# Down projection of a decoder layer: VectorE's order in the fifth and sixth product, and the place of the residual loads

## The chip, the cores and the metric

The kernel runs on one core of a Trainium2 chip. A core has five engines that run on their own and meet only at semaphores: TensorE (PE, matrix products; PEld is its loading of weights), VectorE (DVE), ScalarE (ACT), GpSimd (POOL) and SyncE (SP), which here issues most of the transfers (DMA) between the chip's main memory and the on-chip buffers. The metric is the time of one execution on the device in microseconds; lower is better. Each engine takes its instructions in one written order, so an instruction that waits holds up everything that stands behind it on the same engine.

## The reference, cut to what matters

The layer mixes tokens in two branches (RWKV-7 and S5) and then runs a gated MLP. Only the end of the MLP is touched here: the down projection, the norm behind it, and the residual.

```python
def conv_ffn(h, w_up, conv_w, conv_b, w_down):
    ...
    return (jax.nn.gelu(gate) * val) @ w_down
...
        f = conv_ffn(h, ffn_w_up[l], ffn_conv_w[l], ffn_conv_b[l], ffn_w_down[l])
        x = x + rms_norm(f, norm_ffn_post[l])
```

The hidden width is 2816, the model width 1024, and there are 1024 tokens, all in float32.

## The kernel before, in words

**Seven products.** `down` computes the projection as a two-by-two block product with seven block products instead of eight (Strassen's scheme in Winograd's form). The weights are cut into halves of the hidden width (`kh`, 11 tiles of 128 each) and of the output width (`mh`, 512 columns each), the activations into the same halves of the hidden width and halves of the tokens (`th`, 512 each). The products run in the order `p1, p2, p5, p6, p7, p4, p3`: so p7 is the **fifth product** and p4 the **sixth**, and p3 the seventh. Sums and differences of blocks that the scheme needs are built by VectorE, group by group (`add`, `sub`, lines 1566 and 1569).

**Groups.** Each product runs over the 11 tiles in six groups (`DGROUPS`): two tiles in each, but one tile in the third. A group of two tiles has operands of 128x1024 and 24 matmuls, the half group 128x512 and 12. A product has 132.

**Three matmuls for one.** Every operand is split into a high part (a cast by ScalarE, line 226: `wh` for weights, `xh` for activations) and a low part (VectorE subtracts the cast from the original, line 227: `wl`, `xl`). `step` then issues `xh*wh` (line 1614), `xl*wh` (1615) and `xh*wl` (1616). The operand buffers form a ring of three: the casts of a group wait until TensorE has left the group three before.

**Staging.** Blocks that are needed once are loaded into a ring of four staging buffers (`st`): weight blocks by `a_` (line 1539), activation blocks by `b_` (line 1545). In the fifth product each group loads two, a weight block and an activation block, and VectorE subtracts both (`st<-A,st` and `st<-B,st`) before they are split. A staging buffer is free again when the low part has been taken from it, so the load for a group goes out when `wl` or `xl` of the group two before is done. In the sixth product each group loads two weight blocks: one is split, the other is used by VectorE for `S<-st,S`, an operand of the seventh product.

**Residual.** `resid(th)` loads the residual in eight pieces of 256 KB for each half of the tokens (line 1651): into buffers `T` for the first half, into buffers `A` for the second, as these come free. `outputs` (lines 1660 to 1662) scales, adds the residual and stores; for the first half it runs within the seventh product, for the second after it.

**What sets the order.** TensorE's instructions stay in the order in which they are written. For the other engines a scheduler orders them by its own estimate of when each can start. SP issues all the transfers spoken of here, in one queue and in that order.

Of the kernel before, what the change touches and what calls it, by code (L numbers as in the profile page):

```python
# [9 lines left out]
F32 = mybir.dt.float32  # L10
# [3 lines left out]
ALU = mybir.AluOpType  # L14
# [52 lines left out]
class Kern:  # L67
# [156 lines left out]

    def split(self, hi, lo, x, eng=None):
        self.nc.scalar.copy(hi, x)  # L226
        (eng or self.nc.vector).tensor_tensor(lo, x, hi.bitcast(F32), ALU.subtract)  # L227

    def split_half(self, hi, lo, x, eng=None):

# [1287 lines left out]
    def down(self, dq0, dqf, dqt, dqa, dqs, dqb):  # L1518
# [3 lines left out]
        nc, V, A = self.nc, self.nc.vector, self.nc.scalar  # L1522
        mm = nc.tensor.matmul
        HF = FT // 2
# [3 lines left out]
        def wide(pool, tag, dt=F32, bufs=1):  # L1528
            return pool.tile([128, 1024], dt, tag=tag, name=self.nm(tag), bufs=bufs)

        def cache(tag, g):
            n = len(groups[g])
            pool = {"A": dq0 if g < 4 else dqt, "T": dqt, "S": dqa, "B": dqa if g < 3 else dqb}[tag]
            return pool.tile([128, 512 * n], F32, tag=f"{tag}{g}", name=self.nm(tag), bufs=1)

        def a_(t, mh, kh, g):

            for q, k in enumerate(groups[g]):
                nc.sync.dma_start(t[:, q * 512:q * 512 + 512], self.a["w_down"][kh * HF + k][:, mh * 512:mh * 512 + 512])
            return t  # L1540

        def b_(t, kh, th, g):
# [11 lines left out]
        def operands(g, a, b):  # L1554
            r = ring[0] % 3
            ring[0] += 1
            n = 512 * len(groups[g])
            pool = dqt if r else dq0
            w = [wide(pool, f"w{c}{r}", F32R)[:, :n] for c in "hl"]
            x = [wide(pool, f"x{c}{r}", F32R)[:, :n] for c in "hl"]  # L1560
            self.split(*w, a)
            self.split(*x, b)
            return w, x

        def add(o, x, y):
# [5 lines left out]
        def p1(g):  # L1571
            cA[g], b, cT[g] = a_(cache("A", g), 0, 0, g), b_(stage(g), 0, 0, g), b_(cache("T", g), 0, 1, g)
            o = operands(g, cA[g], b)
            sub(cT[g], cT[g], b)
            return o

        def p2(g):
            o = operands(g, a_(stage(g), 0, 1, g), b_(stage(g), 1, 0, g))
            cS[g] = a_(cache("S", g), 1, 0, g)
            return o  # L1580

        def p5(g):
            add(cS[g], cS[g], a_(stage(g), 1, 1, g))
            o = operands(g, cS[g], cT[g])
            cB[g] = b_(cache("B", g), 1, 1, g)
            sub(cT[g], cB[g], cT[g])
            return o
# [23 lines left out]
        def step(op, q, m, ps, start, stop):  # L1611
            (wh, wl), (xh, xl) = op
            c, x = slice(q * 512 + m * 128, q * 512 + m * 128 + 128), slice(q * 512, q * 512 + 512)
            mm(ps, wh[:, c], xh[:, x], start=start, stop=False, skip_group_check=True)  # L1614
            mm(ps, wh[:, c], xl[:, x], start=False, stop=False, skip_group_check=True)  # L1615
            mm(ps, wl[:, c], xh[:, x], start=False, stop=stop, skip_group_check=True)  # L1616

        def bank(m):
            return self.ps.tile([128, 512], F32, tag=f"d{m}", name=self.nm("d"), bufs=1)

        def product(prep, ps, first, evict, between=lambda g: None):

            for g in range(ng):
                op = prep(g)
                n = len(groups[g])
                qm = [(q, m) for q in range(n) for m in range(4)]
                if g in (0, ng - 1):
                    qm = [(q, m) for m in range(4) for q in range(n)]
                for q, m in qm:
                    step(op, q, m, ps[m], first and g == 0 and q == 0, g == ng - 1 and q == n - 1)  # L1630
                    if g == ng - 1 and q == n - 1:
                        evict(m)
                between(g)
# [9 lines left out]
            acc[th] = sq  # L1643

        def resid(th):
            xs = []
            for m in range(0, NK, 2):
                t = cache("T" if th == 0 else "A", (0, 1, 3, 4)[m // 2])
                for q in range(2):
                    x = t[:, q * 512:q * 512 + 512]  # L1650
                    nc.sync.dma_start(x, self.X1[(m + q) * 128:(m + q) * 128 + 128, th * 512:th * 512 + 512])
                    xs.append(x)
            return xs
# [11 lines left out]
        b, x = [bank(m) for m in range(4)], [bank(4 + m) for m in range(4)]  # L1665
# [33 lines left out]
        def middle(g):  # L1699
            if g == 0:  # L1700
                ss = bank(0)
                self.sumsq(ss, acc[0], True)
                d["y"] = self.rstd(ss, 1e-6, 1.0 / D)
                d["xs"] = resid(0)
            elif g == 1:
                bc = bank(1)
                self.spread(bc, d["y"])
                d["bc"] = dq0.tile([128, 512], F32, tag="bc", name=self.nm("bc"), bufs=1)
                A.copy(d["bc"], bc)
            elif g == 3:  # L1710
                d["xs1"] = resid(1)
        d, last = {}, []
        product(p1, b, True, keep1)
        product(p2, x, True, c11)
        product(p5, x, True, lambda m: None)
        product(p6, b, False, keep2)
        product(p7, b, False, c22)
# [279 lines left out]
```

## Time and profile before

| | |
|---|---|
| timed runs | 1488.09, 1490.83, 1492.19 us; median 1490.83 |
| profiled execution, first to last instruction | 1491.1 us |
| TensorE busy | 1435.8 us (96%) |
| VectorE busy | 1071.2 us (72%) |
| ScalarE busy | 729.8 us (49%) |
| mean granted TensorE clock | 0.984 |
| seven products of the down projection | 1254.9 to 1473.4 us |

For the profiled execution no time other than its span is given; it lies 0.3 us above the median of the runs. Line numbers such as L1569 are those of the kernel before. A wait is read as "engine and line that waited <- engine and line that released it". Names carry no buffer numbers in the profile: `st` is any staging buffer, `d` any of the accumulators of the down projection. A matmul row shows its own length of 0.39 us, but matmuls overlap, so the pace is read from the distance of their starts.

### The profile page before, as it was taken

Reading aid. Unit: us, or ns where it says so; the run is one execution under the profiler, and the core shown is the slowest. Engines: PE = TensorE matmul, PEld = TensorE weight load, DVE = VectorE, ACT = ScalarE, POOL = GpSimd, SP = SyncE. Lnnn points to the kernel's source line nnn. Section 1 sums busy time; section 2 is a strip of 40 time slices with the busy share of each in tenths; the row PEclk is TensorE's granted clock in tenths of the full one; section 3 lists DMA queues with packets and bytes.
Section 4 is the critical chain, followed back from the end, with each engine's and each line's share of the span. In section 5 each row is a group of like instructions: output and inputs, shape, how many; then the busy total and the mean of one; then the engine's idle time right before and its main releaser. Section 6 shows DMA issues by size and latency. Waiting matters only on the chain. (4 is left out here: it accounts for less than half of the span.)

```text
span 1491.1 us, 24155 instructions
## 1 busy us (share of the span) xinstructions
PE 1435.8 (96%) x9284; PEld 1176.3 (79%) x9284; DVE 1071.2 (72%) x1761; ACT 729.8 (49%) x1167; POOL 58.9 (4%) x116
## 2 busy tenths in 40 slices
PE   7999999999999989899999999999999999999996
PEld 5778888778878778677878877888888887888785
DVE  8977765665325859646597798777777777697677
ACT  7677653443324553633554455444444444443351
POOL 0000000010100110100000000000000000000001
PEclk9999999999999999899999999999999999999998
DMA  6453433633511575733374643222222227934723
GB/s 217 121 194 116 129 94 91 212 113 122 164 59 58 171 226 163 189 109 108 121 222 150 205 127 121 85 85 85 85 85 81 76 70 260 328 125 133 236 83 113
DMA packets 121284, 206.26 MB, mean 138 GB/s; under 512 B 29248, under 2 KB 35520, under 8 KB 121168
## 3 DMA queue, kind: packets, MB, share of 16 engines
q1 hardware_dynamic: 113296, 182.43, 39.2%
q0 software_dynamic: 6144, 19.99, 4.0%
q10 hardware_dynamic: 1728, 2.29, 0.4%
q8 instruction: 73, 1.20, 0.4%
q14 instruction: 43, 0.35, 0.1%
HBM read 150.14 MB, written 52.43 MB: 136 GB/s over the span
## 5 line engine op out<-in xcount | busy, mean ns | idle before, releaser
L172 PE MATMUL gm<-hh,wh 128*128 128x512 f32 x672 | 277.0, 412 | 10.5 <-DVE ev L1192 4.3
L173 PE MATMUL gm<-hl,wh 128*128 128x512 f32 x672 | 265.4, 395 | 0.0
L174 PE MATMUL gm<-hh,wl 128*128 128x512 f32 x672 | 265.2, 395 | 0.0
L156 ACT CAST wh<-wf 128x512 fp32r<-128x512 f32 x171 | 105.6, 619 | 168.3 <-PE gm L173 103.8
L157 DVE TENSOR_TENSOR wl<-wf,wh 128x512 fp32r<-128x512 f32 x171 | 116.9, 686 | 77.6 <-ACT wh L156 77.3
L172 PEld LDWEIGHTS gm<-hh,wh 128*128 128x128 f32 x672 | 127.6, 190 | 42.8 <-issue 5.9
L174 PEld LDWEIGHTS gm<-hh,wl 128*128 128x128 f32 x672 | 128.0, 190 | 28.1
L173 PEld LDWEIGHTS gm<-hl,wh 128*128 128x128 f32 x672 | 128.2, 191 | 24.7 <-issue 1.0
L1615 PE MATMUL d<-xl,wh 128*128 128x512 f32 x308 | 121.4, 394 | 3.5 <-DVE xl L227 3.5
L1614 PE MATMUL d<-xh,wh 128*128 128x512 f32 x308 | 121.4, 394 | 2.1 <-ACT xh L226 2.1
L1616 PE MATMUL d<-xh,wl 128*128 128x512 f32 x308 | 121.2, 393 | 0.0
L1440 PE MATMUL rp<-t,h 128*128 128x512 f32 x216 | 84.4, 391 | 1.6 <-ACT p L1454 1.6
L1442 PE MATMUL rp<-t,l 128*128 128x512 f32 x216 | 84.2, 390 | 0.5 <-DVE l L227 0.5
L1441 PE MATMUL rp<-t,h 128*128 128x512 f32 x216 | 84.1, 389 | 0.0
L1615 PEld LDWEIGHTS d<-xl,wh 128*128 128x128 f32 x308 | 58.6, 190 | 16.5 <-DVE xl L227 4.3
L1614 PEld LDWEIGHTS d<-xh,wh 128*128 128x128 f32 x308 | 58.5, 190 | 14.8 <-ACT xh L226 2.5
L1616 PEld LDWEIGHTS d<-xh,wl 128*128 128x128 f32 x308 | 58.6, 190 | 12.2
L226 ACT CAST h<-r 128x1024 fp32r<-128x1024 f32 x34 | 35.8, 1054 | 61.1 <-PE rp L1441 29.6
L227 DVE TENSOR_TENSOR l<-r,h 128x1024 fp32r<-128x1024 f32 x34 | 41.6, 1224 | 29.2 <-ACT h L226 27.7
L1461 DVE SCALAR_TENSOR_TENSOR y<-zv,vecs,y 128x1023 f32<-128x1023 f32 (+1 forms) x36 | 46.1, 1280 | 8.5 <-ACT y L1459 8.5
L1440 PEld LDWEIGHTS rp<-t,h 128*128 128x128 f32 x216 | 40.5, 188 | 11.2 <-ACT p L1454 2.5
L1454 ACT COPY p<-rp 128x512 f32<-128x512 f32 x54 | 31.0, 574 | 36.5 <-PE rp L1442 36.5
(459 smaller groups left out, 3199.4 us busy)
## 6 DMA issues: line engine op xcount, KB each, us to landing
r<-in_w_up_dram SPq DMA_DIRECT2D x36, 512.0 KB, 3.7
wf<-in_w_in_dram SPq DMA_DIRECT2D x62, 256.0 KB, 3.1
st<-in_w_down_dram SPq DMA_DIRECT2D x55, 256.0 KB, 4.1
st<-ACT SPq DMA_DIRECT2D x44, 256.0 KB, 4.5
wf<-in_w_up_dram SPq DMA_DIRECT2D x36, 256.0 KB, 2.9
ACT<-y POOLq DMA_DIRECT2D x18, 512.0 KB, 2.9
GT<-ev SPq DMA_DIRECT2D x32, 256.0 KB, 2.6
wf<-in_w_br_dram SPq DMA_DIRECT2D x32, 256.0 KB, 2.9
```

Of the source, the lines that this page charges most:

```text
L156: nc.scalar.copy(h[:, :n], f[:, :n])
L157: nc.vector.tensor_tensor(l[:, :n], f[:, :n], h[:, :n].bitcast(F32), ALU.subtract)
L172: mm(ps, a, xh[k], start=k == 0, stop=False)
L173: mm(ps, a, xl[k], start=False, stop=False)
L174: mm(ps, b, xh[k], start=False, stop=k == n - 1)
L1440: mm(ps, wh[:, c], xh, start=first and k == 0, stop=False, skip_group_check=True)
L1441: mm(ps, wh[:, c], xl, start=False, stop=False, skip_group_check=True)
L1442: mm(ps, wl[:, c], xh, start=False, stop=k == 3, skip_group_check=True)
L1461: V.scalar_tensor_tensor(y[:, lag:], z[:, 0:1024 - lag], self.vec(nme, i), y[:, lag:], ALU.mult, ALU.add)
L1614: mm(ps, wh[:, c], xh[:, x], start=start, stop=False, skip_group_check=True)
L1615: mm(ps, wh[:, c], xl[:, x], start=False, stop=False, skip_group_check=True)
L1616: mm(ps, wl[:, c], xh[:, x], start=False, stop=stop, skip_group_check=True)
```

## The change

It makes two edits in `down`. First, in the fifth and sixth product every VectorE instruction of a group but the first is put in order behind the last low part (`xl`) of the group before; `issue_after` adds only an order on that one engine, no semaphore. `split` hands back its instruction for this purpose, and `operands` keeps it in `self.lows`. Second, the residual loads are put in SP's order behind the last weight load issued so far (`self.lastw`), which for both halves is that of the sixth product.

```diff
     def split(self, hi, lo, x, eng=None):
         self.nc.scalar.copy(hi, x)
-        (eng or self.nc.vector).tensor_tensor(lo, x, hi.bitcast(F32), ALU.subtract)
+        return (eng or self.nc.vector).tensor_tensor(lo, x, hi.bitcast(F32), ALU.subtract).ins
...
             for q, k in enumerate(groups[g]):
-                nc.sync.dma_start(t[:, q * 512:q * 512 + 512], self.a["w_down"][kh * HF + k][:, mh * 512:mh * 512 + 512])
+                self.lastw = nc.sync.dma_start(t[:, q * 512:q * 512 + 512], self.a["w_down"][kh * HF + k][:, mh * 512:mh * 512 + 512])
             return t
...
             self.split(*w, a)
-            self.split(*x, b)
+            self.lows.append(self.split(*x, b))
             return w, x
...
             for g in range(ng):
-                op = prep(g)
+                with ExitStack() as behind:
+                    if g and prep in (p7, p4):
+                        behind.enter_context(self.tc.issue_after(self.lows[-1]))
+                    op = prep(g)
...
         def resid(th):
+            with self.tc.issue_after(self.lastw.ins):
+                return resid_loads(th)
+
+        def resid_loads(th):
             xs = []
...
-        d, last = {}, []
+        d, last, self.lows = {}, [], []
```

On VectorE, in the fifth product, around its third to fifth group (`st_13294`, `st_13320`, `st_13360` are the weight blocks of these groups in staging, `wl_2409` and `xl_2411` the low parts of the second):

```order
-L1569 TENSOR_TENSOR st_13294<-A_12364,st_13294 128x512
 L227 TENSOR_TENSOR wl_2409_13263<-st_13254,wh_2408_13262 128x1024
 L227 TENSOR_TENSOR xl_2411_13265<-st_13257,xh_2410_13264 128x1024
+L1569 TENSOR_TENSOR st_13294<-A_12364,st_13294 128x512
 L1569 TENSOR_TENSOR st_13296<-B_12862,st_13296 128x512
-L1569 TENSOR_TENSOR st_13320<-A_12391,st_13320 128x1024
 L227 TENSOR_TENSOR wl_2415_13301<-st_13294,wh_2414_13300 128x512
 L227 TENSOR_TENSOR xl_2417_13303<-st_13296,xh_2416_13302 128x512
+L1569 TENSOR_TENSOR st_13320<-A_12391,st_13320 128x1024
 L1569 TENSOR_TENSOR st_13323<-B_12889,st_13323 128x1024
-L1569 TENSOR_TENSOR st_13360<-A_12433,st_13360 128x1024
 L227 TENSOR_TENSOR wl_2421_13329<-st_13320,wh_2420_13328 128x1024
```

Each group's subtraction of the weight block now stands behind both low parts of the group before it; the subtraction of the activation block keeps its place.

On VectorE, in the sixth product, around its third to fifth group (`S_12619`, `S_12647`, `S_12688` are the S blocks of the third, fourth and fifth group; `r` are sums of the product before):

```order
-L1569 TENSOR_TENSOR S_12647<-st_13566,S_12647 128x1024
+L1569 TENSOR_TENSOR S_12619<-st_13540,S_12619 128x512
 L1566 TENSOR_TENSOR r_2438_13440<-r_2438_13440,d_12278 128x512
 L227 TENSOR_TENSOR wl_2454_13533<-st_13530,wh_2453_13532 128x512
 L1566 TENSOR_TENSOR r_2439_13449<-r_2439_13449,d_12279 128x512
 L227 TENSOR_TENSOR xl_2456_13535<-T_12368,xh_2455_13534 128x512
-L1569 TENSOR_TENSOR S_12688<-st_13605,S_12688 128x1024
+L1569 TENSOR_TENSOR S_12647<-st_13566,S_12647 128x1024
 L227 TENSOR_TENSOR wl_2460_13559<-st_13555,wh_2459_13558 128x1024
 L227 TENSOR_TENSOR xl_2462_13561<-T_12397,xh_2461_13560 128x1024
```

Each S subtraction has moved back by one group: it now stands directly ahead of the low parts of its own group instead of the group before.

In SP's queue, at the end of the loads (`X_115` holds the residual, `T_13753` to `T_13762` take the first half of the tokens, `A_13856` to `A_13865` the second):

```order
+L1658 DMA T_13753<-X_115 128x512 x2
+L1658 DMA T_13756<-X_115 128x512 x2
+L1658 DMA T_13759<-X_115 128x512 x2
+L1658 DMA A_13856<-X_115 128x512
+L1658 DMA T_13762<-X_115 128x512 x2
+L1658 DMA A_13856<-X_115 128x512
+L1658 DMA A_13859<-X_115 128x512 x2
+L1658 DMA A_13862<-X_115 128x512 x2
+L1658 DMA A_13865<-X_115 128x512 x2
```

All sixteen now stand together between the last weight load and the first store; before, the A loads stood among the loads of the fifth product and the T loads among those of the sixth. The orders of TensorE, ScalarE and GpSimd are the same as before.

## The prediction

> **What bounds the kernel now.** I read the page's busy shares first, then the windows by product, TensorE's waits, its timeline at those waits, and last the chain of waits, to see what the late instruction had itself waited for.
>
> ```profile
> PE 1435.8 (96%) x9284; PEld 1176.3 (79%) x9284; DVE 1071.2 (72%) x1761; ACT 729.8 (49%) x1167; POOL 58.9 (4%) x116
> ```
>
> TensorE is the bound on the whole; a change elsewhere pays only where TensorE stands still or runs at a lower clock. The windows below are the fifth product, the sixth, the seventh and the tail (start:end, length, busy time of PE, PEld, DVE, ACT, POOL, granted clock, DMA share, GB/s).
>
> ```profile
> 1376.30:1411.90 35.60, 32.13 (x133) 25.77 (x132) 24.78 (x24) 14.21 (x19) 0.00 (x0) 0.95 0.68 212
> 1411.90:1442.00 30.10, 30.10 (x134) 24.96 (x133) 20.96 (x23) 15.20 (x20) 0.00 (x0) 1.00 0.46 153
> 1442.00:1473.40 31.40, 31.38 (x145) 25.75 (x144) 26.06 (x45) 12.15 (x18) 0.00 (x0) 1.00 0.18 68
> 1473.40:1491.10 17.70, 3.90 (x28) 3.42 (x28) 10.76 (x24) 0.63 (x1) 4.59 (x3) 0.64 0.32 119
> ```
>
> The fifth and the sixth product hold the same 132 matmuls, yet the fifth takes 5.5 us more, with idle time and a mean clock of 0.95. From 1300 to 1475 us TensorE has one entry of waits (us in total, times, longest):
>
> ```profile
> PE d L1615 <- DVE xl L227: 3.5, 2, 2.3
> ```
>
> Its timeline (start, duration) gives the two places, and the first matmuls of the fifth, sixth and seventh products:
>
> ```profile
> 1376.32 0.39 PE L1614 MATMUL d<-xh,wh 128*128 128x512 f32 x1
> ...
> 1389.92 0.39 PE L1614 MATMUL d<-xh,wh 128*128 128x512 f32 x1
> 1391.52 0.50 PE L1615 MATMUL d<-xl,wh 128*128 128x512 f32 x1 [1.21 <-DVE xl L227]
> 1391.86 0.39 PE L1616 MATMUL d<-xh,wl 128*128 128x512 f32 x1
> ...
> 1396.87 0.39 PE L1614 MATMUL d<-xh,wh 128*128 128x512 f32 x1
> 1399.52 0.64 PE L1615 MATMUL d<-xl,wh 128*128 128x512 f32 x1 [2.26 <-DVE xl L227]
> ...
> 1403.26 0.39 PE L1615 MATMUL d<-xl,wh 128*128 128x512 f32 x1
> ...
> 1411.90 0.39 PE L1614 MATMUL d<-xh,wh 128*128 128x512 f32 x1
> ...
> 1441.82 0.39 PE L1614 MATMUL d<-xh,wh 128*128 128x512 f32 x1
> ```
>
> The sixth product sets the undisturbed pace: 1441.82 - 1411.90 = 29.92 us, 0.2267 us a matmul, 5.44 us a group of 24, 2.72 us the half group. At the fourth group two steps take 1391.86 - 1389.92 = 1.94 us instead of 0.45: 1.49 us lost. At the fifth group ten steps take 1403.26 - 1396.87 = 6.39 us instead of 2.27: 4.12 us lost, of which the pause is 2.65 - 0.23 = 2.42 and the slow steps after it 1.70. Together 5.61; the whole fifth product (35.58 against 29.92) gives 5.66.
>
> The chain of waits through this stretch (start, us, what) tells why xl was late:
>
> ```profile
> 1377.41 0.33 SPq L1539
> 1377.79 3.67 DMA st<-in_w_down_dram
> ...
> 1382.73 0.70 DVE wl L227
> 1383.44 0.33 SPq L1539
> 1383.83 4.02 DMA st<-in_w_down_dram
> 1387.97 0.06 DVE st L1569
> ...
> 1389.11 1.23 DVE wl L227
> 1390.36 0.33 SPq L1539
> 1390.74 5.11 DMA st<-in_w_down_dram
> 1395.97 0.06 DVE st L1569
> ...
> 1397.11 0.09 DVE wl L227
> 1398.25 1.23 DVE xl L227
> ```
>
> It is a ring: a weight load, the subtraction of that group (L1569), the low half wl of the *preceding* group behind it on VectorE, and only when wl has read its staging buffer the next weight load. One turn per group takes 1389.11 - 1382.73 = 6.38 and 1397.11 - 1389.11 = 8.00 us; TensorE eats a full group in 5.44. So the loads' latency, not VectorE's work, falls behind.
>
> **The change, part by part.** *VectorE's order in the fifth product.* Nothing is added or removed; the first subtraction of each of the second to sixth groups (four wide, one half) moves behind wl and xl of the group before. I follow the new order with durations from these rows (VectorE's starts are then 1.14 apart, ScalarE's casts 1.05 long; a half-width VectorE row is the 0.70 above):
>
> ```profile
> 1367.50 1.23 DVE L1569 TENSOR_TENSOR T<-st,T 128x1024 f32<-128x1024 f32 x1
> 1373.02 1.23 DVE L1569 TENSOR_TENSOR st<-B,st 128x1024 f32<-128x1024 f32 x1 [0.73 <-DMA st<-ACT]
> 1370.90 1.06 ACT L226 CAST wh<-st 128x1024 fp32r<-128x1024 f32 x1 [3.48 <-PE d L1615]
> 1374.41 1.05 ACT L226 CAST xh<-st 128x1024 fp32r<-128x1024 f32 x1 [2.45 <-DVE st L1569]
> ```
>
> From issue to the subtraction a load took 1387.97 - 1383.44 = 4.53 and 1395.97 - 1390.36 = 5.61 us; I take 4.5 and keep 5.6 as the bad end. A cast also waits for TensorE to leave the operand buffers of three groups before (the 3.48 row), that is without pauses for 1381.76, 1387.20, 1389.92 at the fourth, fifth and sixth group.
> First group: wl 1368.7, xl to 1371.0, so the third group's loads go out at 1369.9 and 1371.0. Second: its x subtraction stays at 1373.02 (its load), wl 1374.2 to 1375.4, xl behind the cast of 1374.41 to 1376.7; the fourth group's weight load goes out at 1375.4 instead of 1377.41. Third: subtractions to 1378.0, casts and eviction copies (about 0.6 each, an estimate from half a cast) to 1379.3, wl to 1378.9, xl to 1380.1; the fifth group's weight load goes out at 1378.9 instead of 1383.44. Fourth: subtractions 1380.1 to 1382.5, cast from 1381.9, wl to 1384.2, xl to 1385.4; TensorE needs it at 1390.1, 4.7 us to spare, and the sixth group's weight load goes out at 1384.2 instead of 1390.36. Fifth: its load is there at 1383.4, subtractions to 1387.7, xl to 1390.8, needed at 1395.6. Sixth: subtractions to 1393.1, xl to 1395.7, needed at 1401.0. With 5.6 us loads the fourth group's xl ends at about 1386.1 and the others below 1396.5: still 4 us ahead. So both pauses go, and with them the slow steps: -5.61. Bounds: nothing gained if the loads stay the pace, 5.66 if the product runs at the sixth one's pace; I take the upper, since the spare time is three times the spread of the loads.
>
> What is late next: behind the waiting xl now queue the next group's subtractions, and for them wait the casts. One turn is cast 1.05, wl, xl and the subtraction 1.14 each, some 0.25 of hand-over, 4.7 us: under 5.44.
>
> *The sixth product.* Its S subtractions also move one group later. TensorE waits for nothing there, so there is nothing to gain. The cost is nothing while xl stays ahead: the tightest is the fourth group, whose casts start when the first is left (1406.24 + 5.44 = 1411.68), xl by 1415.2, needed at 1419.9. That cover of 4.7 us gone, TensorE would pause one for one.
>
> *The residual loads.* Sixteen loads of 256 KB leave their places among the weight loads on SP and queue behind the last of these.
>
> ```profile
> 1385.25 4.77 SPq L1651 DMA_DIRECT2D A<-X  x3
> 1425.23 5.60 SPq L1651 DMA_DIRECT2D T<-X  x4
> A<-X SPq DMA_DIRECT2D x8, 256.0 KB, 3.3
> T<-X SPq DMA_DIRECT2D x8, 256.0 KB, 3.8
> 1457.65 0.69 DVE L1661 TENSOR_TENSOR p<-p,T 128x512 f32<-128x512 f32 x1
> ```
>
> The three of 1385.25 held up no issue: the load behind them went out at 1390.36, 0.02 after wl ended. They shared the wires with it, and it took 5.11 us against 3.67 and 4.02, so up to 1.4 us of the second pause is theirs; the order alone covers that, and it is not counted twice. In the new place they begin when the sixth product's last weight loads are out: the buffer of the fourth group's wl is free at 1414.1, so near 1416; the last pair of T buffers waits for that product's fifth xl (about 1420.7), and the A loads queue behind. 4.19 MB at the 153 GB/s that the sixth product's window moved are 27 us (at the fifth's 212, 20): all there by 1436 to 1448. The first is read at 1457.65 - 5.6 = 1452. Hidden: 0. If it came late, VectorE's residual add would stand ahead of the last group's wl and xl.
>
> *The tail.* Its 17.70 us start from the seventh product's last matmuls and move with them; VectorE has 26.06 us of work in the 31.40 of that product and is fed by it. No change.
>
> **Sum.** 1491.1 (the profiled span) - 1.49 - 4.12 = 1485.5; by the whole product 1485.4. The span lies 0.3 above the median 1490.83, so in timed runs 1485.2: I say 1485.3, a gain of 5.5 us or 0.37%. A measurement of this kernel can tell about 0.3% from no change, 4.5 us.
>
> **The rivals.** *The slow stretch is a matter of luck.* The clock in windows of 3.4 us:
>
> ```profile
> 1256.40:1259.80 3.40, 3.40 (x9) 2.65 (x8) 3.40 (x4) 0.00 (x0) 0.00 (x0) 0.50 1.07 388
> 1389.50:1392.90 3.40, 2.19 (x10) 1.51 (x9) 3.10 (x3) 1.05 (x2) 0.00 (x0) 1.00 0.70 208
> 1396.30:1399.70 3.40, 1.14 (x6) 0.64 (x5) 3.40 (x4) 1.04 (x1) 0.00 (x0) 1.00 0.13 13
> 1399.70:1403.10 3.40, 3.40 (x9) 2.63 (x10) 3.26 (x3) 2.01 (x3) 0.00 (x0) 0.50 0.89 272
> ```
>
> A window with 1.14 us of matmul was followed by one at 0.50, a window with 2.19 us was not, and the two slow stretches begin 143.3 us apart, 42 times 3.41. If such windows run on their own phase, a pause split between two of them costs no slow steps. Executions of before would then often lose only 1.49 + 2.42 = 3.9 us, and the gain is 3.9: 1486.9. Against it: the profiled span, with the slow stretch, is 0.3 us from the median. Chance 0.17. (The Trainium skill, TensorE: Matmul & The Clock Gate, "Part 1: The HAM clock gate", describes such a free-running window of about 3.4 us and advises against idle gaps above some 3 us. The spacing of the two stretches agrees; the threshold does not, since 2.26 us of waiting sufficed here. By its threshold the slow steps would not belong to the pause and the sum would be 1487.2.)
>
> *The loads stay the pace.* Over two groups the ring is now load, subtraction 1.2, cast 1.05, wl 1.2 and hand-overs 0.3: 8.25 us at 4.5, 9.35 at 5.6, against 10.88 of two full groups but 8.16 where the half group is one of them. Loads above 7 us would eat the spare time. The moved residuals speak against it: less is on the wires. Half the loss stays: 1488.0. Chance 0.10.
>
> *No effect:* VectorE's order changes as written, but the saved time is given back in the tail. For it speaks only that 17.70 us there are not TensorE's. 1490.8, chance 0.05.
>
> *Slower: the residuals come late.* VectorE's first residual add stands ahead of the seventh product's last wl and xl. Once the first T load lands after 1452, that delay goes on into the end one for one, past some 7 us of spare time (in the old times wl and xl end at 1457.65 + 0.6 + 2.3 = 1460.6, and TensorE's last group begins 5.44 before 1473.4); to end 4.5 us above the old time it must land about 53 us after its issue, where 3.8 us was the median. 1496, chance 0.05.
>
> **How the numbers follow.** The forecast holds 0.63. Its gain is only 1 us above what can be told, so I put 0.57 of it to faster and 0.06 to the same; of the luck rival 0.06 and 0.11, of the pace rival 0.02 and 0.08; no effect 0.05 same; late residuals 0.05 slower. Faster 0.65, same 0.30, slower 0.05. Range: the lowest of the three runs is 2.7 below the median, so 1482.6; up to the pace rival's 1488.0 plus the 1.4 by which the highest run exceeds the median: 1489.4.
>
> **What would show it.** Right: the fifth product lasts 29.9 us at clock 1.00, TensorE's wait for xl is gone, the sixth group's weight load goes out near 1384, the residual loads land between 1416 and 1448, and the tail is still 17.7 us long. Wrong: a wait for xl that stays in the fifth product (pace), a new one in the sixth, VectorE waiting for T<-X in the seventh, or a longer tail.

## The result, and the profile after

The changed kernel takes 1485.28 us (median of 9 runs, 1481.51 to 1486.91) against 1489.68 us for the kernel before in the same comparison (9 runs, 1486.02 to 1492.19): ratio 0.9971, 95% interval 0.996 to 0.9982, a gain of 4.4 us or 0.29%. A second comparison, told below, gave 0.9983 (0.9972 to 0.9995), 2.5 us. The forecast was 1485.3 us and a gain of 5.5 us: the time agrees, the gain came out smaller, on the edge of 0.3% in the first comparison and below it in the second. Why both can be true is told further down.

The windows of the changed kernel, by the same columns as before (start:end, length, busy time of PE, PEld, DVE, ACT, POOL, granted clock, DMA share, GB/s): fifth, sixth and seventh product and the tail.

```profile
1375.94:1405.86 29.92, 29.92 (x133) 24.77 (x132) 25.91 (x27) 13.99 (x19) 0.00 (x0) 1.00 0.71 225
1405.86:1435.78 29.92, 29.92 (x133) 24.77 (x132) 18.66 (x20) 15.03 (x20) 0.00 (x0) 1.00 0.66 216
1435.78:1467.30 31.52, 31.50 (x145) 25.87 (x143) 26.21 (x45) 12.31 (x18) 0.00 (x0) 1.00 0.18 67
1467.30:1485.10 17.80, 3.96 (x28) 3.47 (x28) 10.81 (x24) 0.65 (x2) 4.59 (x3) 0.60 0.32 118
```

The fifth product takes 29.92 us instead of 35.58, at a clock of 1.00 instead of 0.95, and the tail 17.80 instead of 17.70. TensorE's waits from 1250 us to the end (waited <- released, us in total, times, longest) no longer hold one for `xl`:

```profile
PE d L1614 <- ACT xh L226: 2.1, 1, 2.1
PE d L272 <- DVE rsy L139: 2.0, 1, 2.0
```

VectorE's timeline in the fifth product (start, duration) shows the new order, each subtraction behind the `xl` of the group before, and how early `xl` now is. The rows are `wl` and `xl` of the fourth group, the two subtractions of the fifth, and the `xl` of the fifth and of the sixth:

```profile
1382.49 1.22 DVE L227 TENSOR_TENSOR wl<-st,wh 128x1024 fp32r<-128x1024 f32 x1 [0.84 <-ACT wh L226]
1383.63 1.22 DVE L227 TENSOR_TENSOR xl<-st,xh 128x1024 fp32r<-128x1024 f32 x1
1384.76 1.22 DVE L1569 TENSOR_TENSOR st<-A,st 128x1024 f32<-128x1024 f32 x1
1385.90 1.22 DVE L1569 TENSOR_TENSOR st<-B,st 128x1024 f32<-128x1024 f32 x1
...
1389.07 1.22 DVE L227 TENSOR_TENSOR xl<-st,xh 128x1024 fp32r<-128x1024 f32 x1
...
1393.81 1.22 DVE L227 TENSOR_TENSOR xl<-st,xh 128x1024 fp32r<-128x1024 f32 x1
```

The fifth product begins at 1375.94, so TensorE's first matmul with the `xl` of the fourth group comes 61 matmuls of 0.2267 us later, at 1389.77, that of the fifth and sixth group 5.44 us later each, at 1395.21 and 1400.65. `xl` ends at 1384.85, 1390.29 and 1395.03: 4.9, 4.9 and 5.6 us ahead. In these rows no subtraction waits for its load any more; VectorE waits only for ScalarE's cast (0.84 us).

SP's timeline shows the weight loads and, behind them, the residual:

```profile
1375.00 0.81 SPq L1539 DMA_DIRECT2D st<-in_w_down_dram  x2
...
1378.40 0.81 SPq L1539 DMA_DIRECT2D st<-in_w_down_dram  x2
...
1383.74 0.81 SPq L1539 DMA_DIRECT2D st<-in_w_down_dram  x2
...
1389.18 25.24 SPq L1539 DMA_DIRECT2D st<-in_w_down_dram  x22
1414.46 3.00 SPq L1658 DMA_DIRECT2D T<-X  x6
1417.51 0.43 SPq L1658 DMA_DIRECT2D A<-X  x1
1420.19 0.80 SPq L1658 DMA_DIRECT2D T<-X  x2
1421.03 4.32 SPq L1658 DMA_DIRECT2D A<-X  x7
```

The fourth to sixth groups' weight loads go out at 1375.00, 1378.40 and 1383.74 instead of 1377.41, 1383.44 and 1390.36, and the last residual load at 1425.35. Close together they take longer to land than before, 5.2 and 5.9 us at the median instead of 3.8 and 3.3 (DMA issues of the changed kernel from 1374 to 1450 us; the last column is from issue to landing):

```profile
T<-X SPq DMA_DIRECT2D x8, 256.0 KB, 5.2
A<-X SPq DMA_DIRECT2D x8, 256.0 KB, 5.9
```

The last is so there near 1431, well before the seventh product's end, and no engine waits for it in this profile.

### The profile page after: what moved, and what is told of

It reads as the page before. It is cut to its first block, busy times and chain, and to the rows that moved or that the text cites. A ratio compares the mean times of both kernels' runs of the same rounds, so it can differ in the third digit from the quotient of the medians.

```text
span 1485.1 us, 24155 instructions
## 1 busy us (share of the span) xinstructions
PE 1431.1 (96%) x9284; PEld 1172.7 (79%) x9284; DVE 1072.2 (72%) x1761; ACT 729.3 (49%) x1167; POOL 58.8 (4%) x116
```

## The experiments

None of the kernels here leaves out any of the computation. Each was timed beside the kernel before on the same chip, but for the five repetitions of the kernel before, which gave one profile each.

### Which edit does it, and in which product

The four parts alone. **Order only**: the residual loads stay where they were.

```diff
         def resid(th):
-            with self.tc.issue_after(self.lastw.ins):
-                return resid_loads(th)
+            return resid_loads(th)
```

> VectorE's new order alone; the residual loads stay where they were before. Theory (the order breaks the ring of load, subtraction, low half): no wait of TensorE for xl, the fifth product lasts 29.9 us, ratio to before 0.997 as for the whole change. Rival (the residual loads on the wires made the loads late): a pause of 1 us or more stays, the fifth product lasts 31.5 us or more, ratio 0.998 to 1.0.

**Residual loads only**: VectorE's order stays as before.

```diff
-                    if g and prep in (p7, p4):
+                    if False:
                         behind.enter_context(self.tc.issue_after(self.lows[-1]))
```

> The residual loads behind the weight loads alone; VectorE's order as before. Theory (the order): the ring stays, TensorE still waits twice for xl, the second pause at most 1.4 us shorter, fifth product 33 to 35.5 us, ratio 0.998 to 1.0. Rival (the residual loads): fifth product 29.9 us, ratio 0.997.

**Order in the fifth product only**, and **in the sixth only**, both with the residual loads as before.

```diff
-                    if g and prep in (p7, p4):
+                    if g and prep is p7:
```

> VectorE's new order in the fifth product alone; sixth product and residual loads as before. Theory: as the order in both, fifth product 29.9 us and sixth 29.9 us, ratio 0.997; the sixth product's order is worth nothing. Rival (the sixth product's order is needed once its loads start earlier): a wait of TensorE in the sixth product, ratio above 0.998.

```diff
-                    if g and prep in (p7, p4):
+                    if g and prep is p4:
```

> VectorE's new order in the sixth product alone; fifth product and residual loads as before. Theory (two rings, one in each product): the fifth product keeps both pauses, 33 to 36 us, the sixth has none, 29.9 us; ratio 0.998 to 1.0. Rival (the sixth product's order is worth nothing): no difference from before at all, the sixth product with or without a pause as in the two profiles of before.

What was measured, with the lengths of the products and TensorE's waits for `xl` from the profile of each:

| kernel | time, us (runs) | ratio, 95% interval | fifth, us | sixth, us | waits for xl, us |
|---|---|---|---|---|---|
| order only | 1484.46 (12) | 0.9961, 0.9948 to 0.9974 | 29.92 | 29.92 | none |
| residual loads only | 1486.19 (12) | 0.9978, 0.9965 to 0.9991 | 29.92 | 31.41 | 1.19 in the sixth |
| order in the fifth only | 1486.69 (12) | 0.9978, 0.9967 to 0.9988 | 29.92 | 29.92 | none |
| order in the sixth only | 1485.70 (10) | 0.9976, 0.9964 to 0.9987 | 32.81 | 29.92 | 0.20 and 2.05 in the fifth |

The first three and the last had 1489.97 (29 runs) and 1489.53 us (22 runs) for the kernel before beside them. All four intervals overlap that of the whole change, so by the timed runs no part can be told from the whole; what each does is read from its profile, one for each kernel. The order does in each product what it was made for: where it holds, there is no wait for `xl`. The surprise is the second row. With VectorE's order untouched, the fifth product lost both pauses. The chain of waits of that kernel (start, us, what) shows that the ring is still there:

```profile
1372.49 1.23 DVE wl L227
1373.74 0.33 SPq L1539
1374.12 3.29 DMA st<-in_w_down_dram
...
1378.68 0.70 DVE wl L227
1379.39 0.33 SPq L1539
1379.77 3.12 DMA st<-in_w_down_dram
...
1384.15 1.23 DVE wl L227
1385.40 0.33 SPq L1539
1385.77 3.30 DMA st<-in_w_down_dram
...
1390.34 0.98 DVE wl L227
```

The loads take 3.1 to 3.3 us where those of the kernel before took 3.67, 4.02 and 5.11, and the turns 6.19, 5.47 and 6.19 us instead of 6.38 and 8.00 for the last two. The three turns take 17.85 us, TensorE needs 13.60 for the same groups (5.44, 2.72, 5.44). The ring is still the slower, but the lead lasts: this kernel's fifth product begins at 1373.85, and the `xl` of the second group ends 4.7 us before it is needed, that of the fifth group (1392.69, needed at 1393.12) 0.4 us before. So two things together made the fifth product late: the ring, and the residual loads within it, of which six go out between 1370.05 and 1390.02 in the profile of the prediction. Without the ring no `xl` is late; without these loads the ring alone is hidden, but by 0.4 us in the one profile there is. (The Trainium skill, DMA: Bandwidth & Descriptors, "Rules for kernel authors", says of two transfers to disjoint partition halves that they serialize, since both spray across the same 16 DMA engines. That transfers slow each other agrees here: 3.1 to 3.3 us without the residual loads among them, 3.67 to 5.11 with them.)

### How much the kernel before loses

The prediction rests on one execution of the kernel before, so it was profiled five times more, unchanged.

> The kernel before once more, to see how much of the loss is the same in each execution. Theory (the slow stretch behind a pause depends on a phase of its own): the two pauses come again with 2.5 to 4.5 us of waiting in all, the slow steps do not always, the fifth product lasts between 33 and 36 us. Rival (each execution loses the same): 35.6 us again.

> The kernel before a third time. Theory (loads race with the ring, and the slow steps follow a phase of their own): fifth product 33 to 36 us, sixth 29.9 to 31.5 us, with the size of the pauses differing by some tenths of a us between executions. Rival: as the first profile, 35.6 and 29.9 us.

> The kernel before, one more profile. Three profiles of it lost 5.66, 6.38 and 4.38 us in the fifth and sixth product against 29.92 us each. Theory: this is its usual loss, so here again 4 to 6.5 us, and the whole gain of the change comes from there. Rival: the profiles so far were costly ones, and other executions lose 0 to 3 us, which would explain why the timed gain of the changed kernel (4.4 and 2.5 us) lies below 5.5.

> As the look beside it: theory 4 to 6.5 us lost in the fifth and sixth product of the kernel before; rival 0 to 3 us.

> As the two looks beside it: theory 4 to 6.5 us lost in the fifth and sixth product of the kernel before; rival 0 to 3 us.

All profiles in one table, from TensorE's timelines; "lost" is what the fifth and sixth product take above 29.92 us each.

| profile | span, us | first product starts | first, us | fifth, us | sixth, us | pauses for xl, us | lost, us |
|---|---|---|---|---|---|---|---|
| before, that of the prediction | 1491.1 | 1254.94 | 31.62 | 35.58 | 29.92 | 1.21, 2.26 | 5.66 |
| before, second | 1493.7 | 1256.76 | 31.66 | 35.11 | 31.11 | 0.79, 2.19; 0.90 in the sixth | 6.38 |
| before, third | 1493.4 | 1258.60 | 31.62 | 32.19 | 32.03 | 1.63; 1.74 in the sixth | 4.38 |
| before, fourth | 1490.0 | 1254.34 | 31.64 | 35.14 | 29.92 | 0.75, 2.26 | 5.22 |
| before, fifth | 1490.0 | 1254.86 | 31.66 | 34.72 | 30.02 | 0.40, 2.18 | 4.90 |
| before, sixth | 1484.0 | 1250.92 | 30.04 | 34.11 | 29.92 | 1.94 | 4.19 |
| changed | 1485.1 | 1254.57 | 31.61 | 29.92 | 29.92 | none | 0 |
| changed, again | 1482.1 | 1251.61 | 31.64 | 29.92 | 29.92 | none | 0 |
| order only | 1478.7 | 1249.36 | 30.04 | 29.92 | 29.92 | none | 0 |

The kernel before loses 4.2 to 6.4 us, 5.1 on average, in all six; the rival that most executions lose 0 to 3 us is refuted for profiled ones. From the start of the first product to the end it takes 235.3 us on average, the changed kernel 230.5 both times: 4.8 us. (Most of the difference to 5.1 comes from the first product, which lasted only 30.04 us in one of the six and 31.6 in both profiles of the changed kernel.) Most of a span's spread is where the first product starts: 1249.36 to 1258.60 us, in work that the change does not touch, almost twice the gain. About half of that is the clock: the traces of the table have 4 to 9 stretches of 3.41 us at a granted clock of 0.50 ahead of the first product, and with 1.7 us taken off for each the starts lie within 4.0 us instead of 9.2.

The sixth product of the second profile shows that the prediction's "nothing to gain" there was the luck of one execution. VectorE's timeline (the third group is the half one, its `wl` is 128x512; behind it come `wl` and `xl` of the fourth):

```profile
1419.61 1.23 DVE L1569 TENSOR_TENSOR S<-st,S 128x1024 f32<-128x1024 f32 x1 [4.11 <-DMA st<-in_w_down_dram]
...
1421.35 0.69 DVE L227 TENSOR_TENSOR wl<-st,wh 128x512 fp32r<-128x512 f32 x1
...
1424.63 1.22 DVE L1569 TENSOR_TENSOR S<-st,S 128x1024 f32<-128x1024 f32 x1 [1.39 <-DMA st<-in_w_down_dram]
1425.77 1.22 DVE L227 TENSOR_TENSOR wl<-st,wh 128x1024 fp32r<-128x1024 f32 x1
1426.91 1.22 DVE L227 TENSOR_TENSOR xl<-T,xh 128x1024 fp32r<-128x1024 f32 x1
```

It is the same fault as in the fifth product: a subtraction that belongs to a later group waits 4.11 us for its load, and the low parts that TensorE needs stand behind it. The load had taken 7.08 us. In the kernel with the residual loads moved but the old order, a load of 6.26 us stands in the chain that ends in the 1.19 us pause, although no residual load was out then: the 22 weight loads of the sixth product went out in a row, and that these crowd each other is likely but not shown.

The profile that the prediction read shows how near this was (kernel before, the subtraction of the fifth group and the `xl` of the fourth):

```profile
1421.70 1.23 DVE L1569 TENSOR_TENSOR S<-st,S 128x1024 f32<-128x1024 f32 x1 [2.01 <-DMA st<-in_w_down_dram]
...
1423.98 1.22 DVE L227 TENSOR_TENSOR xl<-T,xh 128x1024 fp32r<-128x1024 f32 x1
```

This `xl` ends at 1425.20; the product begins at 1411.90, so TensorE needs it 61 matmuls later, at 1425.73: 0.5 us to spare. In the changed kernel the same `xl` ends 5.0 us ahead.

### The slow steps behind a pause

Two of these profiles answer the rival on the clock. TensorE's timeline behind the pause at the fifth group (start, length of one; the pace is the distance of the starts), first in the sixth profile of the kernel before:

```profile
1390.11 0.39 PE L1614 MATMUL d<-xh,wh 128*128 128x512 f32 x1
1392.44 0.58 PE L1615 MATMUL d<-xl,wh 128*128 128x512 f32 x1 [1.94 <-DVE xl L227]
1392.81 0.63 PE L1616 MATMUL d<-xh,wl 128*128 128x512 f32 x1
1393.24 0.63 PE L1614 MATMUL d<-xh,wh 128*128 128x512 f32 x1
...
1396.19 0.39 PE L1615 MATMUL d<-xl,wh 128*128 128x512 f32 x1
```

and in the kernel with the order in the sixth product only:

```profile
1392.22 0.39 PE L1614 MATMUL d<-xh,wh 128*128 128x512 f32 x1
1394.66 0.50 PE L1615 MATMUL d<-xl,wh 128*128 128x512 f32 x1 [2.05 <-DVE xl L227]
1395.00 0.39 PE L1616 MATMUL d<-xh,wl 128*128 128x512 f32 x1
1395.23 0.39 PE L1614 MATMUL d<-xh,wh 128*128 128x512 f32 x1
```

A pause of 1.94 us was followed by 3.4 us of slow steps (eight from 1392.81 to 1396.19), one of 2.05 us by none. So it is not the length alone that decides. Of the six profiles before, five have the slow steps in the fifth product (about 1.7 us each), only the third has none. The same holds at the start of the first product: TensorE waits there 2.05 or 2.06 us in every profile told of so far, and its first product then takes 31.6 us in eight of them and 30.0 in four. (The Trainium skill, TensorE: Matmul & The Clock Gate, "Part 1: The HAM clock gate", says that the activity window of about 3.4 us runs freely and that the count of slow matmuls differs from run to run for that reason. This agrees. It also wants an idle window of that length before the clock falls; here 1.94 us of waiting were enough.)

What decides is where the pause falls. In each trace the stretches at half clock begin whole multiples of 3.413 us apart: in the first profile of the kernel before, the one in the first product and the one in the fifth are 42 of these apart, 143.36 us. The windows of the two pauses just shown, and the ones behind them (columns as in the windows of the changed kernel), first the 1.94 us, then the 2.05 us:

```profile
1389.31:1392.72 3.41, 1.47 (x7) 0.93 (x6) 3.41 (x4) 1.04 (x1) 0.00 (x0) 1.00 0.13 23
1392.72:1396.13 3.41, 3.41 (x9) 2.65 (x9) 3.16 (x3) 2.26 (x3) 0.00 (x0) 0.50 0.86 293
```

```profile
1390.92:1394.33 3.41, 1.69 (x8) 1.07 (x6) 3.22 (x3) 1.04 (x1) 0.00 (x0) 1.00 0.03 10
1394.33:1397.74 3.41, 3.08 (x13) 2.55 (x14) 3.31 (x4) 1.61 (x2) 0.00 (x0) 1.00 0.86 273
```

The first pause lies in one window and leaves TensorE busy for 1.47 us of it, and the next window runs at 0.50; the second reaches over the edge, leaves 1.69 us, and the clock stays. So it is in all fourteen traces of this case, in the windows from 1240 us to the end of the seventh product: all 13 with at most 1.47 us of busy time were followed by one at 0.50, none of those with 1.67 us or more was. (In earlier stages, with other matmuls, windows with up to 2.8 us of busy time were followed by half clock too, so the bound holds for these products only.) A pause of about 2 us thus costs 1.7 us more or nothing, by its place.

### The pause that is left, and a faster kernel

One pause of TensorE is left in the down projection, 2.06 us at the start of the first product. Two ways to it were tried. **Accumulators of the stage before**: the pool of the preceding stage stays open and the down projection takes its accumulators from there, so that no change of pools has to wait for VectorE's last sum of that stage.

```diff
         def bank(m):
-            return self.ps.tile([128, 512], F32, tag=f"d{m}", name=self.nm("d"), bufs=1)
+            return self.rp() if m < 2 else self.chp()
...
-        b, x = [bank(m) for m in range(4)], [bank(4 + m) for m in range(4)]
+        b = [bank(m) for m in range(4)]
+        x = [t[:, k:k + 512] for t in (self.mmp(), self.mmp()) for k in (0, 512)]
...
-                        self.ps = tops.enter_context(tc.tile_pool(name="psd", **psum))
+                        self.ps = outer.enter_context(tc.tile_pool(name="psd", **psum))
...
-                    self.ps = pool("psw", space=PSUM)
```

> The changed kernel, and in addition the down projection takes its accumulators from the pool of the stage before instead of a new one, so that its first matmul no longer waits for VectorE's last sum of that stage (the 2.1 us pause at the start of the first product). Theory: the pause goes and with it the slow steps that follow it in some executions (first product 29.9 to 30.1 us instead of 31.6), 2 to 3.7 us less than the changed kernel, ratio to before 0.9945 to 0.9958. Rival (the pause moves on to the second group, whose low part xl comes 3 us later): at most 1 us less, ratio 0.9965 or above.

1490.77 us (12 runs), ratio 1.0008 (0.9996 to 1.002): the whole gain of the change is lost. The pause at the start is gone, but TensorE's waits (from 1250 us on) show what came in its place:

```profile
PE mm L1614 <- DVE p L1566: 3.7, 2, 2.9
...
PE mm L1614 <- DVE q L1566: 1.8, 2, 1.0
PE rp L1615 <- DVE xl L227: 1.0, 1, 1.0
```

Four of the accumulators are now the halves of two tiles of 1024 columns. All four waits for `p` and `q` stand in the last group of the second and of the seventh product, where a matmul into the second half of a tile waits until VectorE has read the finished sum in the first half. The 1.0 us is the second group's `xl` in the first product, which the pause had covered: the rival came true as well, but is the smaller part.

**The sum earlier**: beside the change, VectorE takes the last sum that the first accumulators wait for (`zg`, line 1470) ahead of a multiply-add of the convolution of that stage's other half (line 1461; not a subtraction, as the expectation calls it).

```diff
-            V.tensor_tensor(d["gate"][:, 512:], d["u2"], d["c"], ALU.add)
-            va = conv2(d["val"], FT + i)
+            zg = V.tensor_tensor(d["gate"][:, 512:], d["u2"], d["c"], ALU.add).ins
+            with ExitStack() as behind:
+                if i == FT - 1:
+                    behind.enter_context(self.tc.issue_after(zg))
+                va = conv2(d["val"], FT + i)
```

> The changed kernel, and one sum more of the preceding stage moved ahead on VectorE: the last sum that the down projection's first accumulators wait for (line 1470) no longer stands behind a subtraction of that stage's other half. Theory: TensorE's 2.06 us pause at the start of the first product shrinks to about 0.9, and the half-clock steps that follow it in most profiles (first product 31.6 instead of 30.0 us) become rarer; 1 to 2.5 us less than the changed kernel, 1482.5 to 1484.5 us, ratio to the kernel before 0.9955 to 0.9965. Rival: what is moved behind the sum makes the second group's low half xl late, and TensorE waits for that in place of the pause; gain at most 0.5 us, ratio 0.997.

The changed kernel itself ran beside it, unchanged:

> The changed kernel once more, beside the one with the early sum. If its fifth and sixth products run at TensorE's pace in this execution too, they last 29.9 us each, without a wait for xl; the forecast and the rivals then differ only in how much the kernel before loses on average. Theory: ratio 0.997, 4 to 5 us. By the rival that half of the gain seen was the spread between executions: ratio 0.9985.

With the earlier sum 1483.28 us (12 runs), ratio 0.9966 (0.9953 to 0.9979); the changed kernel 1485.47 us (11 runs), ratio 0.9983 (0.9972 to 0.9995); the kernel before 1487.98 us (23 runs). The changed kernel's profile is as the theory had it, its ratio in timed runs is that of the rival, 0.9985. TensorE's waits from 1250 us on in the kernel with the earlier sum:

```profile
PE d L272 <- DVE rsy L139: 2.0, 1, 2.0
PE d L1617 <- DVE zg L1470: 0.9, 1, 0.9
```

The pause shrinks from 2.06 to 0.9 us, and the first product takes 30.14 us instead of 31.64, without a new wait. That is 1.2 + 1.5 = 2.7 us by the two profiles and 2.2 by the medians, as the theory had it (its ratio came out just above 0.9955 to 0.9965), though the two intervals still overlap a little; by its median it beats both kernels. That the slow steps have gone for good is one profile's word, since they were missing in others by luck; but a pause of 0.9 us leaves 2.5 us of busy time in its window, more than the 1.67 us from which on none followed in these products.

## Why the prediction was right, point by point

**What bounds the kernel: right.** With `xl` in time the fifth product runs at the sixth one's pace to the hundredth (29.92 us). The ring was read rightly too: from the third group on no subtraction of the fifth product waits for a load in the first profile of the changed kernel, and in the second a single one does, for 0.5 us.

**VectorE's order in the fifth product, -5.61: the mechanism right, its steps within 0.5 us.** The weight loads were to go out at 1375.4, 1378.9 and 1384.2 and went out at 1375.00, 1378.40 and 1383.74, in an execution whose fifth product began 0.38 us earlier. `xl` was to be 4.7 to 5.3 us ahead and was 4.9 to 5.6. The size, 5.61, was that of one execution; six average 5.1, the sixth product included.

**The sixth product, "nothing to gain": wrong.** Two of the six profiles lost 1.19 and 2.11 us there, at the fourth group that the prediction named as the tightest, and the kernel with the residual loads alone lost 1.49. The step had taken the absence of a wait in one execution for slack; its own profile had 0.5 us there. On its own the order in this product was worth 3.8 us by the medians, more than the sixth product lost in any profile (2.11 us). Most of this goes with the clock: the ten runs of that kernel have a mean granted clock of 0.988, the 22 of the kernel before beside it 0.986. One stretch of 3.41 us at 0.50 takes 0.0011 off the mean clock of 1490 us and costs 1.7 us, so the difference is worth some 3 us (an estimate from these figures). Why these runs had fewer such stretches, by luck or by the edit, stays open.

**The residual loads, 0: right in the sum, wrong in the share.** "Up to 1.4 us of the second pause is theirs" was too little: without them both pauses of the fifth product were gone. Since the order alone removes these as well (order in the fifth only: no pause), not counting them twice was right. The landing, hidden until the seventh product, and the tail came as told; VectorE waits for no residual load in either profile of the changed kernel, and the rival of late residuals is refuted.

**The base and the sum: two errors that cancel.** The prediction took the span of 1491.1 us for a time 0.3 above the median. A run's time is about 1.75 us more than its span: 1486.85 and 1485.1 in the profiled run of the changed kernel, 1495.47 and 1493.7 in the second of the kernel before. So the profiled execution took some 1492.9 us, 3.2 above the median of the nine runs, 1489.68. Taking 5.6 off a time would have given 1487.3. The median of three that the forecast leaned on was 1.1 us high, and the gain that it subtracted was 1.1 us larger than the one measured; these two gave 1485.3. That the time agrees to 0.02 us is luck.

**Why the gain in timed runs is 4.4 and 2.5 us and not 5.** The profiles show 4.8 us from the first product's start on. The runs of one kernel spread over 5 to 10 us, and by the profiles their first product starts anywhere in 9 us. The first interval (ratio 0.996 to 0.9982, or 2.7 to 6.0 us) holds the 4.8, the second (0.7 to 4.2 us) does not. In the second the runs of the kernel before had the higher mean clock (0.9869 against 0.9864), by the same estimate some 0.7 us in their favour. Whether executions without a kept profile lose less in the fifth product cannot be seen here and stays open.

**The rivals.** Luck of the slow stretch: its mechanism, windows with a phase of their own, is shown, but the luck is rarer than it had it, since five of six profiles have the slow steps in the fifth product. Loads as the pace: refuted, no `xl` waited; loads above 7 us, which it named, did not occur in the changed kernel, where the longest took 5.5. No effect and late residuals: refuted by the ratio and by VectorE's waits. The chances put 0.65 on faster by over 0.3%; measured were 0.29% and 0.17%, both within 0.3%, to which it had given 0.30. What made that likelier was visible: a forecast of 5.5 us with a bound of 4.5 needed the loss of one execution to be the usual one.

## What to carry to other kernels

When an in-order engine both consumes loads and frees the buffers for the next ones, put what the matrix engine needs soon ahead of what waits for a load; here this made loads of up to 5.6 us harmless, with the residual loads among them or not. A product without a wait in one profile may have no slack at all: look at how late its operands are, and profile the kernel before more than once where the gain is below the spread of its runs. Compare times with times: a span is not a time, and the constant between them was 40% of this gain.

## What the hardware showed unexpectedly

A wait of 1.94 us on TensorE was followed by 3.4 us at half clock and one of 2.05 us was not; whether the same 2.06 us wait costs 1.6 us more differed from execution to execution. In the windows of 3.413 us by which the clock changes, 1.47 us of busy time or less was always followed by half clock in the products of the down projection, 1.67 us or more never. The weight loads of 256 KB in the chains of the fifth product took 3.1 to 3.3 us without residual loads among them and up to 5.11 us with them; of the 22 of the sixth product single ones took 6.26 and 7.08 us, where the median was 3.6 and 4.0. The work ahead of the down projection, the same in all the kernels of the table, ended anywhere between 1249 and 1259 us.
